# Retention queries of a hybrid decoder layer by seven products that are summed in PSUM

## The chip, the cores and the metric

The kernel runs on one core of one Trainium2 chip. The metric is device time of one execution in microseconds (us), the median of several runs. The core's engines are TensorE (PE in the profile; its weight loads are PEld), VectorE (DVE), ScalarE (ACT), GpSimd (POOL) and SyncE (SP), which here issues DMAs. Each works through its own instructions in order, and semaphores hold an instruction back until what it needs is there.

## The reference

One decoder layer for 512 tokens of width 1024, with 16 learned tokens put in front. Retention, stick-breaking attention and two gates share one input projection; a SwiGLU feed-forward follows. The part that the change touches is the projection of the retention's queries and their rotation:

```python
proj = hn @ w_in                                   # (528, 1024) @ (1024, 11264)
rq, rk, rv, rg, sq, sk, sv, ga, gb = jnp.split(proj, ...)
q_r = rotary(heads(rq, 4), pos) * (256 ** -0.5)    # 4 heads of 256
k_r = rotary(heads(rk, 4), pos)
y_ret = head_groupnorm(retention_chunkwise(q_r, k_r, heads(rv, 4)))
y_ret = (silu(rg) * merge_heads(y_ret)) @ w_ret_out
```

Everything is float32. The queries of a head are a product of 256 x 1024 (weights, transposed) by 1024 x 512 (tokens).

## The kernel before

**Numbers in two parts.** Each operand is held as a high and a low part (`wh`, `wl` for weights, `hT`, `hL` for the normalised tokens), made by `split` (L103): a ScalarE copy into the matmul type and a VectorE subtraction for the rest. A product is then three matmul passes: high by high, high by low, low by high. Weights come from DRAM into `raw` (4 buffers, L120) and are split into `wh`/`wl` (5 pairs, L81); both are reused in turn, so a load waits for a split, and a split waits until TensorE is through with an earlier pair.

**Products of two forms.** `feat_mm` (L142) multiplies weights by tokens with the weights as the stationary operand: for 1024 input rows, 8 row blocks and 3 passes, 24 matmuls into one bank. `seven` (L263) computes a product that is cut in 2 x 2 quarters by seven smaller products in place of eight (Strassen's scheme as Winograd ordered it): it needs sums of weight quarters, s1 to s4, which GpSimd makes (L230 or L258), and sums of token quarters, t1 to t4, which are made once and kept in `th`, `tl`. The retention's values and gate (`tok_seven`, L297) and most of the feed-forward (`feat_seven`, L287) are done so; the partial results are brought together by VectorE in a tile `ub` of SBUF. `feat_quarters` (L221) loads the weights of `feat_seven` in two tiles, makes S1, S2, S3, S4 from them in tiles `x` (S2, S3) and `y` (S1, S4), and splits raw1, x, y and A22, the second half of raw2.

**The retention stage** runs over 4 heads (L1111). `ret_qk` (L990) multiplies the queries: for each half e of the head's 256 columns, `feat_mm` over the 512 tokens into one bank of a pair `pa`. `rotate` (L971) reads the two banks by VectorE and splits the results. Then the keys, over 528 tokens in two pieces of 264 columns, per half e. After that come the scores (`ret_scores`), the gate (`ret_gate`), the weighted values (`ret_pv`), the transposition (`ret_T`), the next head's values (`rv_proj`) and the output projection of this head (`ret_out`, 96 matmuls of 512 columns into banks `pp`). For head 0, `ret_out` copies its banks to `acc` by ScalarE (L1105); for heads 1 and 2 VectorE adds them (L1108).

**What sets the order.** The program is written in the order above, but a scheduler places the instructions on each engine, interleaving what is independent; parts are pinned. So the output projection of head h - 1 stands among the queries and keys of head h, and the gate's first products among the keys. PSUM has pools of two banks `pp`, two `pb`, and two pairs `pa` in this stage.

Of the kernel before, what the change touches and what calls it, by code (L numbers as in the profile page):

```python
# [10 lines left out]
F32 = mybir.dt.float32  # L11
# [23 lines left out]
def hybrid_block(  # L35
# [37 lines left out]
    def bank_a():  # L73
        return ps_a.tile([P, 2, 512], F32, tag="a", name="pa")
# [19 lines left out]
    def mm(*args, **kw):  # L94
        return keep(nc.tensor.matmul(*args, **kw))  # L95
# [43 lines left out]
        cn = src.shape[1]  # L139
        return load_units(src, kn, cn, [(0, kn, c, P) for c in range(0, cn, P)])  # L140

    def feat_mm(dst, unit, xh, xl, kn=KD):  # L142

        wh, wl = unit
        for k in range(kn):
            mm(dst, wh[:, k, :], xh(k), start=(k == 0), stop=False)
            mm(dst, wh[:, k, :], xl(k), start=False, stop=False)
            mm(dst, wl[:, k, :], xh(k), start=False, stop=(k == kn - 1))

    def tok_mm(dst, units, xh, xl, first=True, last=True, k0=0):  # L150

# [63 lines left out]
    def wun_split(v):  # L215
        wh = wun.tile([P, v.shape[1], v.shape[2]], F32R, tag="wh", name="wh")
        wl = wun.tile([P, v.shape[1], v.shape[2]], F32R, tag="wl", name="wl")
        split(wh, wl, v)
        return wh, wl

    def feat_quarters(src, sums, pin=False):  # L221

        raw1, raw2 = raw_of(src[:, 0:P]), raw_of(src[:, P:])
        A11, A12 = raw1[:, 0:KH, :], raw1[:, KH:KD, :]
        A21, A22 = raw2[:, 0:KH, :], raw2[:, KH:KD, :]
        x = sums.tile([P, KD, P], F32, tag="st", name="st")
        y = sums.tile([P, KD, P], F32, tag="st", name="st")
        S1, S2, S3, S4 = y[:, 0:KH, :], x[:, 0:KH, :], x[:, KH:KD, :], y[:, KH:KD, :]
        for d, p, q, op in ((S1, A21, A22, ALU.add), (S2, S1, A11, ALU.subtract), (S3, A11, A21, ALU.subtract), (S4, A12, S2, ALU.subtract)):
            ins = nc.gpsimd.tensor_tensor(d, p, q, op=op)  # L230
            if pin:
                tc.keep_in_program_order(ins)
        f, g = slice(0, KH), slice(KH, KD)
        a, b, c, d = wun_split(raw1), wun_split(x), wun_split(y), wun_split(A22)
        cut = lambda u, k: (u[0][:, k, :], u[1][:, k, :])
        return dict(a11=cut(a, f), a12=cut(a, g), s2=cut(b, f), s3=cut(b, g), s1=cut(c, f), s4=cut(c, g), a22=d)

# [25 lines left out]
    def seven(product, bank1, bank2, ub, after=lambda n: None):  # L263


        n = ub.shape[-1]
        p1 = bank1()
        product(0, p1)
        nc.scalar.activation(ub[:, 1, :], p1, AF.Copy)
        p = bank2()  # L270
        product(1, p[:, 0, :])
        after(1)
        product(2, p[:, 1, :])
        nc.vector.tensor_tensor(ub[:, 0:2, :], p, ub[:, 1:2, :].to_broadcast([P, 2, n]), op=ALU.add)
        p = bank1()
        product(3, p)
        nc.vector.tensor_tensor(ub[:, 2, :], p, ub[:, 1, :], op=ALU.add)
        p = bank1()
        product(4, p)
        nc.vector.tensor_tensor(ub[:, 1:4:2, :], p.rearrange("p (o n) -> p o n", o=1).to_broadcast([P, 2, n]), ub[:, 1:3, :], op=ALU.add)  # L280
        p = bank2()
        product(5, p[:, 0, :])
        product(6, p[:, 1, :])
        after(6)
        nc.vector.tensor_tensor(ub[:, 1:3, :], p, ub[:, 1:3, :], op=ALU.add)
# [11 lines left out]
    def tok_seven(u, tok, ub, **kw):  # L297


        def product(n, dst):  # L300
            a, b = PRODUCTS[n]
            xh, xl = tok.operand(b)
            wh, wl = u[a]
            for s in range(2):
                ts_ = slice(s * P, (s + 1) * P)
                tok_mm(dst[:, s * 256 : (s + 1) * 256], [(wh, wl)], lambda k: xh(k)[:, ts_], lambda k: xl(k)[:, ts_])

        one = iter([bank_p, bank_p, bank_b])
        seven(product, lambda: next(one)(), bank_a, ub, **kw)


    hpool = ctx.enter_context(ExitStack())
# [675 lines left out]
        return s4.tile([P, L], F32R, tag="qk", name="qk", bufs=8)  # L988

    def ret_qk(h):  # L990
        uq = feat_units(w_in[:, O_RQ + DK * h : O_RQ + DK * (h + 1)])
        pq = bank_a()
        for e in range(2):
            feat_mm(pq[:, e, :], uq[e], xtok, ltok)
        q = [(qk_tile(), qk_tile()) for _ in range(2)]
        idf = lambda t: t[:, :T]
        rotate(pq[:, 0, :], pq[:, 1, :], cosT[:, NM:], sinT[:, NM:], idf, [(a[:, :T], b[:, :T]) for a, b in q])
        uk = feat_units(w_in[:, O_RK + DK * h : O_RK + DK * (h + 1)])
        pks = []
        for e in range(2):  # L1000
            pk = bank_a()
            for i in range(2):
                cs = slice(264 * i, 264 * (i + 1))
                feat_mm(pk[:, i, :264], uk[e], lambda k: hT[:, k, cs], lambda k: hL[:, k, cs])
            pks.append(pk[:, :, :264])
        k = [(qk_tile(), qk_tile()) for _ in range(2)]
        two = lambda t: t.rearrange("p (a b) -> p a b", a=2)
        rotate(pks[0], pks[1], two(cosT), two(sinT), two, [(two(a), two(b)) for a, b in k])
        return q, k
# [381 lines left out]
```

## Time and profile before

| | |
|---|---|
| median of 3 runs | 1178.73 us (1178.39 to 1178.78) |
| the profiled execution | 1178.72 us, span 1176.9 us |
| matmuls in the span | 7529 |
| granted TensorE clock, mean | 0.999 |
| retention, query projection of head 0 | from 355.30 us on |
| feed-forward, seven-product part | about 860 to 1040 us |

A row of the page's groups has the line, engine and operation, output <- inputs by the program's names, partitions x elements, the count, then busy time in us, the mean of one in ns, and the idle time of the engine before these instructions with what ended it. A row of the timeline has start and length in us, then the instruction and a count, with idle time and its ender in brackets. A row of windows has, for each engine, busy us and the number of instructions, then the granted clock, the DMA share and GB/s. A row of one line's or tile's instructions has the shortest, the median and the longest duration in ns.

### The profile page before, as it was taken

To read this page: it belongs to the slowest core of one execution; us is meant where nothing else is said; L and a number is where in the kernel's file an instruction comes from. 1 tells how busy PE (TensorE), PEld (TensorE's weight loads), DVE (VectorE), ACT (ScalarE), POOL (GpSimd) and SP (SyncE) were. 2 spreads that over 40 slices of the span, in tenths; PEclk is the share of its full clock that TensorE was granted. 3 is DMA by queue.
4 is the path that set the end of the run, shared out by engine and by line. 5 is a ranking of instruction groups with operands and counts; after the bars stand their busy time and mean duration, and the time that the engine had idled before them with its cause. 6 is when DMAs were issued, how large, how long until landed. Compare 5 with 4: busy or idle time off the path is not lost.

```text
span 1176.9 us, 18856 instructions
## 1 busy us (share of the span) xinstructions
PE 1164.9 (99%) x7529; PEld 1056.3 (90%) x7529; DVE 844.0 (72%) x1120; ACT 532.1 (45%) x899; POOL 333.5 (28%) x358
## 2 busy tenths in 40 slices
PE   9999999999999999999999999999999999999997
PEld 7988999988899998998899898888999999998886
DVE  7488888888577873786586567767799998773333
ACT  6476666666233434434243334335455444442321
POOL 2021112126644403320240200001356676610000
PEclk9999999999999999999999999999999999999999
DMA  7332122222641323115122434344033333353311
GB/s 235 99 99 74 62 72 64 77 77 92 194 148 60 93 90 114 55 53 154 36 82 82 133 90 134 126 160 126 19 108 108 109 108 108 108 162 101 97 36 72
DMA packets 146536, 118.25 MB, mean 100 GB/s; under 512 B 3832, under 2 KB 135168, under 8 KB 146448
## 3 DMA queue, kind: packets, MB, share of 16 engines
q1 hardware_dynamic: 145856, 115.85, 32.5%
q8 instruction: 59, 0.97, 0.4%
q10 hardware_dynamic: 592, 1.20, 0.3%
q14 instruction: 29, 0.24, 0.1%
HBM read 109.96 MB, written 7.08 MB: 99 GB/s over the span
## 4 chain that ended last, share of the span: by engine, by line
PE 92%; DVE 5%; issue 1%; ACT 1%; DMA 0%; POOL 0%; POOLq 0%; DVEq 0%; ACTq 0%
PE pp L95 41%; PE pb L95 20%; PE pa L95 20%; PE pc L95 5%; PE px L95 3%; PE pb L98 3%; DVE wl L101 1%; DVE sm L603 1%; ACT wh L104 1%; DVE sl L101 0%; DMA ysb<-in_x_dram 0%; DVE al L101 0%; DVE kl L101 0%; DVE qb L101 0%; DVE qa L101 0%
## 5 line engine op out<-in xcount | busy, mean ns | idle before, releaser
L101 DVE TENSOR_TENSOR wl<-raw,wh 128x1024 fp32r<-128x1024 f32 x196 | 260.7, 1338 | 60.3 <-ACT wh L104 59.3
L104 ACT ACTIVATE wh<-raw 128x1024 fp32r<-128x1024 f32 x194 | 195.2, 1014 | 203.4 <-PE pa L95 59.5
L95 PE MATMUL pp<-hT,wh 128*128 128x512 f32 (+1 forms) x304 | 112.0, 369 | 0.0
L95 PE MATMUL pp<-hL,wh 128*128 128x512 f32 (+1 forms) x304 | 107.7, 354 | 0.0
L95 PE MATMUL pp<-hT,wl 128*128 128x512 f32 (+1 forms) x304 | 107.6, 354 | 0.0
L258 POOL TENSOR_TENSOR st<-raw 128x512 f32<-128x512 f32 x28 | 44.4, 1608 | 170.3 <-DMA raw<-in_w_in_dram 170.3
L101 DVE TENSOR_TENSOR wl<-st,wh 128x1024 fp32r<-128x1024 f32 x54 | 75.1, 1392 | 13.1 <-ACT wh L104 12.1
L95 PE MATMUL pp<-qk,wh 128*128 128x512 f32 x256 | 80.1, 394 | 0.0
L230 POOL TENSOR_TENSOR st<-raw 128x512 f32<-128x512 f32 x40 | 61.1, 1528 | 50.3 <-DVE wl L101 50.3
L95 PE MATMUL pp<-wh,hT 128*128 128x256 f32 (+1 forms) x240 | 73.9, 309 | 0.1
L95 PE MATMUL pp<-wl,hT 128*128 128x256 f32 (+1 forms) x240 | 73.0, 305 | 0.7 <-DVE wl L101 0.4
L95 PE MATMUL pp<-wh,hL 128*128 128x256 f32 (+1 forms) x240 | 73.0, 305 | 0.2 <-DVE hL L101 0.2
L104 ACT ACTIVATE wh<-st 128x1024 fp32r<-128x1024 f32 x54 | 56.6, 1056 | 35.6 <-PE pp L95 15.6
L95 PE MATMUL pa<-hL,wh 128*128 128x264 f32 (+1 forms) x208 | 66.2, 318 | 0.0
L95 PE MATMUL pa<-hT,wh 128*128 128x264 f32 (+1 forms) x208 | 66.2, 318 | 0.0
L95 PE MATMUL pa<-hT,wl 128*128 128x264 f32 (+1 forms) x208 | 66.1, 318 | 0.0
L603 DVE TENSOR_TENSOR_SCAN sm<-sm,mask 128x528 f32<-128x528 f32 (+1 forms) x64 | 54.8, 857 | 14.3 <-ACT sm L600 13.5
L95 PEld LDWEIGHTS pp<-hT,wl 128*128 128x128 f32 x304 | 57.2, 188 | 8.4
L613 POOL CAST mg<-sp 128x32 fp32r<-128x32 f32 x32 | 7.5, 233 | 197.6 <-DVE sp L604 153.7
L95 PEld LDWEIGHTS pp<-hT,wh 128*128 128x128 f32 x304 | 57.3, 188 | 5.8
L95 PEld LDWEIGHTS pp<-hL,wh 128*128 128x128 f32 x304 | 57.4, 189 | 5.3
L95 PEld LDWEIGHTS pp<-qk,wh 128*128 128x128 f32 x256 | 47.7, 188 | 10.7
(346 smaller groups left out, 3680.3 us busy)
## 6 DMA issues: line engine op xcount, KB each, us to landing
raw<-in_w_in_dram SPq DMA_DIRECT2D x88, 512.0 KB, 4.2
raw<-in_w_ffn_in_dram SPq DMA_DIRECT2D x44, 512.0 KB, 3.8
raw<-in_w_ffn_out_dram SPq DMA_DIRECT2D x22, 512.0 KB, 3.6
raw<-in_w_ret_out_dram SPq DMA_DIRECT2D x16, 512.0 KB, 3.4
raw<-in_w_sb_out_dram SPq DMA_DIRECT2D x8, 512.0 KB, 3.9
raw<-in_w_out_dram SPq DMA_DIRECT2D x8, 512.0 KB, 4.0
ysb<-in_x_dram SPq DMA_DIRECT2D x4, 512.0 KB, 7.1
gb_d<-go SPq DMA_DIRECT2D x8, 256.0 KB, 2.0
```

What stands on the lines that cost most here:

```text
L95: return keep(nc.tensor.matmul(*args, **kw))
L98: return keep(nc.tensor.transpose(dst, src, idn))
L101: return nc.vector.tensor_tensor(lo, src, hi.bitcast(F32), op=ALU.subtract)
L104: ins = nc.scalar.activation(hi, src, AF.Copy)
L230: ins = nc.gpsimd.tensor_tensor(d, p, q, op=op)
L258: nc.gpsimd.tensor_tensor(d[:, k : k + 2], p[:, k : k + 2], q[:, k : k + 2], op=op)
L603: nc.vector.tensor_tensor_scan(rev, rev, mask[:, r0:][:, ::-1], 0.0, op0=ALU.mult, op1=ALU.max)
L613: nc.gpsimd.tensor_copy(g[:, two, 0:NM], m)
```

## The change

The queries alone go over to seven products; the keys stay as they were. `ret_qk` loads the query weights by `feat_quarters`, with the sums y (S1, S4) split ahead of x (S2, S3), and calls a new function, `feat_chain`. This does not bring the partial results together in SBUF with an add for each, as `seven` does. It lets TensorE go on adding into the same PSUM bank ("a" or "b") and copies the bank out by ScalarE at each point at which the running sum is one of the quarters or a part of one: bank "a" holds a11 b11, then with s2 t2, then with s3 t3, then with a22 t4. Bank "b" holds s1 t1, then with s4 b22. The product a12 b21 has a bank of its own. The results are four quarters of a SBUF tile `ub` (the one buffer that `seven` also uses), from which `rotate` now reads. The first half of the keys, `keys(0)`, is written between the products, the second after the queries' rotation.

```diff
-    def feat_mm(dst, unit, xh, xl, kn=KD):
+    def feat_mm(dst, unit, xh, xl, kn=KD, first=True, **kw):
 
         wh, wl = unit
         for k in range(kn):
-            mm(dst, wh[:, k, :], xh(k), start=(k == 0), stop=False)
-            mm(dst, wh[:, k, :], xl(k), start=False, stop=False)
-            mm(dst, wl[:, k, :], xh(k), start=False, stop=(k == kn - 1))
+            mm(dst, wh[:, k, :], xh(k), start=(first and k == 0), stop=False, **kw)
+            mm(dst, wh[:, k, :], xl(k), start=False, stop=False, **kw)
+            mm(dst, wl[:, k, :], xh(k), start=False, stop=(k == kn - 1), **kw)
...
-        a, b, c, d = wun_split(raw1), wun_split(x), wun_split(y), wun_split(A22)
+        a = wun_split(raw1)
+        if s1_first:
+            c, b = wun_split(y), wun_split(x)
+        else:
+            b, c = wun_split(x), wun_split(y)
+        d = wun_split(A22)
...
+    def feat_chain(u, tok, q, u22, beside=None):
+        banks = {}
+
+        def product(name, bank, more=False):
+            a, b = name
+            feat_mm(banks[bank], u[a], *tok.operand(b), KH, first=not more, skip_group_check=True)
+
+        def add(d, p):
+            nc.vector.tensor_tensor(d, p, d, op=ALU.add)
+
+        (q11, q12), (q21, q22) = [[q[:, e, H * t : H * (t + 1)] for t in range(2)] for e in range(2)]
+
+        def rest():
+            banks["c"] = bank_p()[:, :H]
+            product(("a12", "b21"), "c")
+            add(q11, banks["c"])
+
+        banks["a"] = bank_a()[:, 0, :H]
+        product(("a11", "b11"), "a")
+        nc.scalar.activation(q11, banks["a"], AF.Copy)
+        if beside:
+            rest()
+        banks["b"] = bank_p()[:, :H]
+        product(("s1", "t1"), "b")
+        nc.scalar.activation(q22, banks["b"], AF.Copy)
+        product(("s2", "t2"), "a", True)
+        nc.scalar.activation(q12, banks["a"], AF.Copy)
+        product(("s4", "b22"), "b", True)
+        add(q12, banks["b"])
+        product(("s3", "t3"), "a", True)
+        nc.scalar.activation(u22, banks["a"], AF.Copy)
+        add(q22, u22)
+        (beside or rest)()
+        product(("a22", "t4"), "a", True)
+        nc.scalar.activation(q21, banks["a"], AF.Copy)
...
     def ret_qk(h):
-        uq = feat_units(w_in[:, O_RQ + DK * h : O_RQ + DK * (h + 1)])
-        pq = bank_a()
-        for e in range(2):
-            feat_mm(pq[:, e, :], uq[e], xtok, ltok)
+        uq = feat_quarters(w_in[:, O_RQ + DK * h : O_RQ + DK * (h + 1)], s4, s1_first=True)
+        uk = feat_units(w_in[:, O_RK + DK * h : O_RK + DK * (h + 1)])
+        pks = []
+
+        def keys(e):
+            pk = bank_a()
+            pks.append(pk[:, :, :264])
+            for i in range(2):
+                cs = slice(264 * i, 264 * (i + 1))
+                feat_mm(pk[:, i, :264], uk[e], lambda k: hT[:, k, cs], lambda k: hL[:, k, cs])
+
+        pq = s4.tile([P, 4, 512], F32, tag="ub", name="ub", bufs=1)
+        feat_chain(uq, tokens, pq, pq[:, 2, :H], lambda: keys(0))
...
-        uk = feat_units(w_in[:, O_RK + DK * h : O_RK + DK * (h + 1)])
-        pks = []
-        for e in range(2):
-            pk = bank_a()
-            for i in range(2):
-                cs = slice(264 * i, 264 * (i + 1))
-                feat_mm(pk[:, i, :264], uk[e], lambda k: hT[:, k, cs], lambda k: hL[:, k, cs])
-            pks.append(pk[:, :, :264])
+        keys(1)
```

How the change moves instructions, at three places. First TensorE in head 0, right behind the values of that head; before, the first matmul of each block (`wh_4186` and `wh_4190` are the two halves of the query weights, `wh_4265` and `wh_4269` those of the keys, `pp_4501` is the gate):

```order
L95 MATMUL pa_4194<-hT_83,wh_4186 128x512
L95 MATMUL pa_4194<-hT_83,wh_4190 128x512
L95 MATMUL pa_4273<-hT_83,wh_4265 128x264
L95 MATMUL pp_4501<-wh_4397,hT_83 128x256
L95 MATMUL pa_4322<-hT_83,wh_4269 128x264
```

and after, again the first matmul of each block (`pa_4221` is bank "a", `pp_4249` bank "b", `pp_4235` bank "c"; `wh_4192` holds a11 and a12, `wh_4196` y, `wh_4200` x, `wh_4204` a22; `pa_4303` and `wh_4212` are the first half of the keys, `pa_4383` the second):

```order
L95 MATMUL pa_4221<-hT_83,wh_4192 128x256
L95 MATMUL pp_4235<-hT_83,wh_4192 128x256
L95 MATMUL pp_4249<-th_94,wh_4196 128x256
L95 MATMUL pa_4303<-hT_83,wh_4212 128x264
L95 MATMUL pa_4221<-th_94,wh_4200 128x256
L95 MATMUL pp_4249<-hT_83,wh_4196 128x256
L95 MATMUL pa_4221<-th_94,wh_4204 128x256
L95 MATMUL pp_4562<-wh_4458,hT_83 128x256
L95 MATMUL pa_4383<-hT_83,wh_4216 128x264
```

Two blocks of 24 matmuls of 512 columns became seven of 12 of 256. The 48 of the first key half are spread among them: 2 stand ahead of s2 (`wh_4200`), 10 behind it, 2 ahead of s3, 34 ahead of a22.

Second, ScalarE in head 0, after, from the first key split to the last copy out of bank "a" (L337, L342, L344, L348 and L352 are the five copies of `feat_chain`; `rvm` and `vs` belong to the learned tokens' values; `wh_4458` to `wh_4480` are the gate's weights):

```order
L104 ACTIVATE wh_4212<-raw_4208 128x1024
L1000 ACTIVATE vs_3952<-pb_4149 16x256
L337 ACTIVATE ub_4220<-pa_4221 128x256
L104 ACTIVATE wh_4216<-raw_4210 128x1024
L104 ACTIVATE rvm_3886<-vs_3952 16x512
L342 ACTIVATE ub_4220<-pp_4249 128x256
L1011 ACTIVATE rvm_3886<-rvm_3886 16x512
L344 ACTIVATE ub_4220<-pa_4221 128x256
L348 ACTIVATE ub_4220<-pa_4221 128x256
L104 ACTIVATE wh_4476<-st_4466 128x1024
L104 ACTIVATE wh_4480<-st_4467 128x1024
L352 ACTIVATE ub_4220<-pa_4221 128x256
```

Before, no copy of the queries stood in this queue. Now each stands behind a split or a copy of something else, the first behind the key split and two value copies, the last behind two splits of the gate's sums (`st`).

Third, VectorE in head 2, where the output projection of head 1 (`acc`) stands among the queries' weights; before (`raw_6240` and `raw_6242` are the two query tiles):

```order
L1108 TENSOR_TENSOR acc_3901<-pp_6130,acc_3901 128x512
L101 TENSOR_TENSOR wl_6181<-raw_6174,wh_6180 128x1024
L101 TENSOR_TENSOR wl_6245<-raw_6240,wh_6244 128x1024
L101 TENSOR_TENSOR vl_6092<-ub_5873,vh_6091 128x2x256 x2
L101 TENSOR_TENSOR wl_6249<-raw_6242,wh_6248 128x1024
L958 TENSOR_TENSOR vs_5874<-pb_6071,vs_5874 16x256
L1108 TENSOR_TENSOR acc_3901<-pp_6144,acc_3901 128x512
L1108 TENSOR_TENSOR acc_3901<-pp_6158,acc_3901 128x512
L101 TENSOR_TENSOR rvm_3886<-vs_5874,rvm_3886 16x512
```

and after (`wl_6377` is y's low half, `wl_6381` x's; L1153 is the add that was L1108):

```order
L1153 TENSOR_TENSOR acc_3901<-pp_6252,acc_3901 128x512
L101 TENSOR_TENSOR wl_6303<-raw_6296,wh_6302 128x1024
L101 TENSOR_TENSOR wl_6373<-raw_6362,wh_6372 128x1024
L101 TENSOR_TENSOR vl_6214<-ub_5995,vh_6213 128x2x256 x2
L1001 TENSOR_TENSOR vs_5996<-pb_6193,vs_5996 16x256
L1153 TENSOR_TENSOR acc_3901<-pp_6266,acc_3901 128x512
L101 TENSOR_TENSOR wl_6377<-st_6367,wh_6376 128x1024
L101 TENSOR_TENSOR rvm_3886<-vs_5996,rvm_3886 16x512
L1153 TENSOR_TENSOR acc_3901<-pp_6280,acc_3901 128x512
L101 TENSOR_TENSOR wl_6381<-st_6366,wh_6380 128x1024
L1153 TENSOR_TENSOR acc_3901<-pp_6306,acc_3901 128x512
```

The fourth add (`pp_6158`, now `pp_6280`) followed the third directly; now the low half of y, which waits for GpSimd's sums by way of ScalarE, and the learned tokens' values stand ahead of it.

2 lines of the change are left out of this document (1 added, 1 removed).

## The prediction, made before the changed kernel had run

> **What bounds the kernel now.** I read the page first, then the windows of the retention stage, then single rows where the change acts.
>
> ```profile
> span 1176.9 us, 18856 instructions
> PE 1164.9 (99%) x7529; PEld 1056.3 (90%) x7529; DVE 844.0 (72%) x1120; ACT 532.1 (45%) x899; POOL 333.5 (28%) x358
> PE 92%; DVE 5%; issue 1%; ACT 1%; DMA 0%; POOL 0%; POOLq 0%; DVEq 0%; ACTq 0%
> core 0: us, PE busy (x) PEld busy (x) DVE busy (x) ACT busy (x) POOL busy (x), PEclk, DMA share, GB/s
> 355.00:640.00 285.00, 284.79 (x1924) 262.00 (x1923) 204.70 (x260) 111.18 (x151) 81.52 (x60) 1.00 0.27 83
> ```
>
> TensorE (PE) is busy 99% of the span, and carries 92% of the chain that ended last. The last row is a stretch of some three retention heads: TensorE stands still for 0.2 of 285 us, at full granted clock. So matmul time taken out shortens the run one for one, and any new wait of TensorE lengthens it one for one. Each other engine has room there on average (VectorE 80 us, ScalarE 174, GpSimd 203); only the moment at which something is ready can cost.
>
> **The matmuls.** Their durations mislead, so I count from start to start.
>
> ```profile
> L95 PE MATMUL pa<-hT,wh 128*128 128x512 f32 x64 | 25.2, 393 | 0.0
> 355.30 0.39 PE L95 MATMUL pa<-hT,wh 128*128 128x512 f32 x1
> 366.41 0.28 PE L95 MATMUL pa<-hT,wh 128*128 128x264 f32 x1
> L95 PE MATMUL pb<-nT,wh 128*128 128x256 f32 x144 | 40.6, 282 | 0.0
> 860.00:1040.00 180.00, 180.00 (x1511) 180.00 (x1510) 162.77 (x159) 83.87 (x103) 116.49 (x72) 1.00 0.36 106
> ```
>
> The query projection of head 0 begins at 355.30 and the keys at 366.41: 48 matmuls of 512 columns in 11.11 us, 231 ns each. The window in the feed-forward stage holds only matmuls of 256 columns, in the same seven-product form: 1511 in 180.00 us, 119.1 ns each. The new projection has 7 products x 4 row blocks x 3 passes = 84 of these: 10.0 us. **Saved: 11.11 - 10.0 = 1.1 us a head, 4.4 us in four heads.** The keys keep their 96 matmuls a head; they are only cut into pieces around the products.
>
> The Trainium skill (TensorE: Matmul & The Clock Gate, Back-to-back issue gap and LDWEIGHTS) speaks against this: in a stream of weight loads and matmuls the spacing is set by both, and a load costs its columns over 1.2, 107 ns for 128. Were that load added to each matmul, 36 more loads a head would eat the saving, an estimate of 3.9 us by that page against 1.1. The trace differs: 1510 loads stand beside the 1511 matmuls at 119 ns, so the load is in that figure already.
>
> **The other work.** Per head the change adds four GpSimd operations of 512 elements, 3.5 splits of 1024 in place of 2, five ScalarE copies of 256 out of PSUM and three VectorE adds of 256.
>
> ```profile
> L230 POOL TENSOR_TENSOR st<-raw x40: 1285/1674/1759, 828.2 to 1030.4; 128x512 f32<-128x512 f32 x40
> L230 POOL TENSOR_TENSOR st<-st,raw x20: 1282/1296/1622, 829.5 to 1029.2; 128x512 f32<-128x512 f32 x20
> L230 POOL TENSOR_TENSOR st<-raw,st x20: 1739/2278/2299, 832.8 to 1032.1; 128x512 f32<-128x512 f32 x20
> L101 DVE TENSOR_TENSOR wl<-st,wh 128x1024 fp32r<-128x1024 f32 x54 | 75.1, 1392 | 13.1 <-ACT wh L104 12.1
> L104 ACT ACTIVATE wh<-st 128x1024 fp32r<-128x1024 f32 x54 | 56.6, 1056 | 35.6 <-PE pp L95 15.6
> L269 ACT ACTIVATE ub<-pp 128x512 f32<-128x512 f32 x6 | 3.6, 597 | 0.1
> L957 ACT ACTIVATE vs<-pb 16x256 f32<-16x256 f32 x5 | 1.8, 370 | 0.1
> L277 DVE TENSOR_TENSOR ub<-pp,ub 128x512 f32<-128x512 f32 x6 | 4.1, 686 | 0.1
> ```
>
> GpSimd's sums, the same four operations as in the feed-forward stage: 2 x 1.67 + 1.30 + 2.28 = 6.9 us (minima 5.6, maxima 7.4). ScalarE: 1.5 x 1.06 for splits and five copies. A copy of 256 columns is not in the trace; it lies between 0.37 (256 on 16 partitions) and 0.60 (512), and I take 0.60, since that row too reads 128 partitions of PSUM. Together 4.6 us. VectorE: 1.5 x 1.39 + 3 x at most 0.69 = 4.2. All of this lies beside TensorE on average; the question is the places where TensorE waits for it.
>
> **Head 0** has no output projection of an earlier head to fill in. Here I replay the chain.
>
> ```profile
> 339.86 0.40 SPq L121 DMA_DIRECT2D raw<-in_w_in_dram  x1
> DMA to landing us min/median/max: 4.9/5.1/5.4
> 351.84 0.69 DVE L101 TENSOR_TENSOR vl<-ub,vh 128x512 fp32r<-128x512 f32 x1 [0.70 <-ACT vh L104]
> 353.94 1.22 DVE L285 TENSOR_TENSOR ub<-pa,ub 128x1024 f32<-128x1024 f32 x1
> 355.41 1.14 ACT L104 ACTIVATE vh<-ub 128x512 fp32r<-128x512 f32 x2
> ```
>
> The second weight tile is issued at 339.86 and lands by 345.3 (the landings of that stretch); 6.9 of sums give 352.2. ScalarE splits y (S1 and S4) by 353.2, a value copy and x (S2 and S3) follow by 354.9. VectorE's low halves of y, of a value quarter and of x, then the last sum of the values (1.22) end at 357.9. Behind it ScalarE has two value copies (1.14), the key split (1.06), a meta copy (0.37) and then q11's copy out of bank "a", which is done at about 361.1. TensorE, from 355.30, has a11, a12 and s1, 36 matmuls, and two of the keys: ready for s2 on bank "a" at 359.8. **It waits 1.2 us** (nothing if the sums take their minima; up to 3 if VectorE is held up too). The other hand-overs have a product or a piece of keys (1.4 us or more) to cover a copy of 0.6.
>
> **Heads 1 to 3** have the output projection of the head before among the chain. Its sums are taken out of two banks by ScalarE (head 1) or by VectorE's adds (heads 2, 3), and the new splits stand ahead of these in both queues.
>
> ```profile
> 541.08 0.37 SPq L121 DMA_DIRECT2D raw<-in_w_in_dram  x1
> raw<-in_w_in_dram SPq DMA_DIRECT2D x88, 512.0 KB, 4.2
> 544.42 1.21 DVE L285 TENSOR_TENSOR ub<-pa,ub 128x1024 f32<-128x1024 f32 x1
> 546.15 0.68 DVE L1108 TENSOR_TENSOR acc<-pp,acc 128x512 f32<-128x512 f32 x1
> 549.88 0.63 PE L95 MATMUL pp<-qk,wh 128*128 128x512 f32 x2
> ```
>
> Head 2: issue 541.08, landing 545.3, sums 552.2, y split 553.3, its low half 554.6, the meta values' low half 555.3, the fourth add 556.0. TensorE began that fourth product (12 matmuls) at 549.88. Now, from 549.7: 12 of these, 10 of a11, 12 of the fifth, 2 of s2, and at 556.6 the sixth product wants that bank: 0.6 spare. The third add comes, by the same queue (1.21, 0.69, 0.68, two splits, two value halves, 0.41, 0.68), at 552.3 and is wanted at 553.6. So I take no wait, with 0 to 1.8 as bounds (next part).
>
> **Sum**, against the profiled execution's own 1178.72 (span 1176.9 and 1.8 around it; the median of the runs shown is 1178.73): -4.4 + 1.2 = -3.2, **1175.5 us**.
>
> **Rivals.**
>
> *VectorE loses time to GpSimd's new sums.*
>
> ```profile
> 352.79 1.23 DVE L101 TENSOR_TENSOR wl<-raw,wh 128x1024 fp32r<-128x1024 f32 x1 [0.26 <-ACT wh L104]
> 354.59 3.53 POOL L258 TENSOR_TENSOR st<-raw 128x512 f32<-128x512 f32 x2 [16.98 <-DMA raw<-in_w_in_dram]
> 356.89 3.47 DVE L101 TENSOR_TENSOR vl<-ub,vh 128x512 fp32r<-128x512 f32 x2
> 358.08 3.44 POOL L258 TENSOR_TENSOR raw<-raw 128x512 f32<-128x512 f32 x2
> 360.29 2.31 DVE L101 TENSOR_TENSOR wl<-raw,wh 128x1024 fp32r<-128x1024 f32 x1
> ```
>
> With GpSimd idle a value half takes 0.69 and a weight half 1.23; beside GpSimd's rows two of the first take 3.47 and one of the second 2.31: 3.2 us lost in 5.7. The skill (SBUF — State Buffer, Who interferes with whom) gives the reason: a VectorE instruction with two SBUF inputs contends with a GpSimd instruction that reads SBUF, one with at most one does not. The trace agrees. In head 2 just such halves fill VectorE's queue from 545.3 on. A loss of 3.1 puts the third add at 555.4, 1.8 late. With this in heads 2 and 3 and head 0's 1.2: 1178.7 - 4.4 + 4.8 = **1179.1**. Against it: in the window of the feed-forward stage the same sums run every 10 us beside a VectorE at 90%, the weight halves average 1.39, and TensorE never stops.
>
> *A bank copy behind a split that waits for GpSimd (slower).* In head 0 the last copy, q21's, stands in ScalarE's queue behind two splits of the gate's weights, the first of which needs six of GpSimd's pieces.
>
> ```profile
> L258 POOL TENSOR_TENSOR st<-raw x28: 1283/1302/2332, 354.6 to 666.9; 128x512 f32<-128x512 f32 x28
> ```
>
> The gate's second tile takes the slot of the second query tile, free at about 358.6; it lands at 362.8. Six pieces at 1.30 end at 370.6, two splits and the copy at 373.3. TensorE wants that bank, for the second half of the keys, at 355.3 + 10.0 + 5.9 (keys) + 1.2 + 2.9 (24 of the gate) = 375.3. At the maximum, 2.33, the pieces end at 376.8 and the copy at 379.5: 4.2 late. It decides from 1.64 a piece on. Heads 1 to 3 lie between 0 and 4.2 each; I take 0.8, near the low end, since there 96 matmuls of the output projection (22 us at 231 ns) run among the chain and give GpSimd that much more time: 1178.7 - 4.4 + 1.2 + 4.2 + 2.4 = **1182.1**.
>
> *The durations are the cost.* 84 x 0.282 against 48 x 0.393 would be 4.8 us more a head, **1198**. The starts quoted above exclude it nearly.
>
> **How the numbers follow.** Forecast 1175.5: 0.55. VectorE's loss, 1179.1: 0.33. Copy behind the split, 1182.1: 0.11. Durations: 0.01. Faster by over 0.2% (2.4 us, about what a measurement of this kernel can tell from no change) is the first, 0.55; within it the second, 0.33; slower the last two, 0.12. The range runs from no wait at all (1174.3, and 0.4 for the spacing's own uncertainty) to the first rival: 1173.9 to 1179.2. Within the forecast alone it is 1173.9 to 1176.4.
>
> **What would show it.** The query chain's matmuls at 119 ns from start to start; TensorE idle before s2 in head 0, ended by ScalarE's copy into ub, about 1 us; none before the output projection's products in heads 2 and 3. There, a wait ended by the add into acc, with weight halves of 2 us ahead of it, is the first rival; a wait before the second half of the keys, ended by the last copy into ub, the second. A spacing well over 119 ns in the chain would make the saving itself wrong.

## The result, and the profile after

The changed kernel takes **1185.18 us** (median of 4 runs, 1184.73 to 1185.55), beside 1178.76 (1178.39 to 1178.86) for the kernel before on the same chip: a ratio of 1.0055, 95% interval 1.0037 to 1.0072. The forecast was 1175.5. The profiled execution took 1185.55 us.

The page of the changed kernel, its span, its engines and the shares of the chain that ended last:

```profile
span 1183.8 us, 19227 instructions
PE 1163.2 (98%) x7673; PEld 1060.5 (90%) x7673; DVE 884.6 (75%) x1140; ACT 545.7 (46%) x927; POOL 365.9 (31%) x374
PE 78%; DVE 12%; issue 4%; ACT 2%; DMA 2%; POOL 2%; POOLq 0%; DVEq 0%; ACTq 0%
```

TensorE's busy time fell by 1.7 us, and yet the span grew by 6.9. VectorE (DVE) has 40.6 us more, and its share of the chain went from 5% to 12%. What TensorE waited for between 350 and 740 us, the retention heads (engine, tile and line <- who ended the wait: us in total, number, the longest). Before, this view is empty for the same stretch. After:

```profile
PE pp L95 <- DVE acc L1153: 2.5, 2, 1.3
PE pb L95 <- DVE qk L101: 1.7, 1, 1.7
PE pa L95 <- DVE wl L101: 1.1, 1, 1.1
PE pa L95 <- DVE rt L1025: 1.0, 2, 0.9
PE pp L95 <- ACT wh L104: 0.5, 1, 0.5
PE pb L95 <- ACT qk L104: 0.2, 1, 0.2
PE pa L95 <- ACT ub L337: 0.2, 1, 0.2
```

Of 7.2 us of waits VectorE ended 6.3, at four kinds of place: the add of the output projection into `acc` (heads 2 and 3), the low half of a rotated key ahead of the scores (head 1), a low half of query weights (head 1), and the rotation, which holds a bank pair. The last row is the wait that was forecast for head 0, at a sixth of its size.

The list shows too little of each wait. The record of a matmul of 256 columns lasts 0.28 us and the next one starts 0.12 us after it, so the first 0.16 us of a stop count as busy, and a short stop does not show at all. Counted from start to start (all that is over 0.1 us above the usual spacing), TensorE loses 11.5 us between 350 and 740 us, and lost 1.0 before.

Two whole heads (1 and 2) from the first matmul of head 1 that reads `xm` to the first of head 3, as a row of windows, before and then after:

```profile
433.67:641.54 207.87, 207.79 (x1378) 189.85 (x1377) 142.20 (x182) 79.79 (x108) 52.74 (x40) 1.00 0.28 84
```

```profile
435.53:647.43 211.90, 207.07 (x1449) 192.07 (x1448) 165.04 (x192) 86.99 (x122) 68.51 (x48) 1.00 0.27 83
```

VectorE has ten instructions more here, which at its mean of before (142.20 / 182 = 0.78) would be 7.8 us; it has 22.8 us more. What grew is seen in the timeline of head 2, before and then after: the head's first `xm` matmul, as a marker, and VectorE's rows some ten us behind it.

```profile
537.71 0.28 PE L95 MATMUL pb<-wh,xm 128*48 128x256 f32 x1
...
545.55 0.68 DVE L101 TENSOR_TENSOR vl<-ub,vh 128x512 fp32r<-128x512 f32 x1
546.75 2.35 DVE L101 TENSOR_TENSOR wl<-raw,wh 128x1024 fp32r<-128x1024 f32 x2
549.01 1.28 DVE L101 TENSOR_TENSOR vl<-ub,vh 128x512 fp32r<-128x512 f32 x2
551.35 0.41 DVE L958 TENSOR_TENSOR vs<-pb,vs 16x256 f32<-16x256 f32 x1
551.69 0.67 DVE L1108 TENSOR_TENSOR acc<-pp,acc 128x512 f32<-128x512 f32 x1
```

```profile
541.97 0.28 PE L95 MATMUL pb<-wh,xm 128*48 128x256 f32 x1
...
549.80 1.76 DVE L101 TENSOR_TENSOR vl<-ub,vh 128x512 fp32r<-128x512 f32 x1
551.49 0.68 DVE L1153 TENSOR_TENSOR acc<-pp,acc 128x512 f32<-128x512 f32 x1
552.09 3.95 DVE L101 TENSOR_TENSOR wl<-raw,wh 128x1024 fp32r<-128x1024 f32 x2
555.96 2.39 DVE L101 TENSOR_TENSOR vl<-ub,vh 128x512 fp32r<-128x512 f32 x2
558.27 0.41 DVE L1001 TENSOR_TENSOR vs<-pb,vs 16x256 f32<-16x256 f32 x1
558.61 0.67 DVE L1153 TENSOR_TENSOR acc<-pp,acc 128x512 f32<-128x512 f32 x1
```

Beside these stand GpSimd's new sums (L230), and behind the last add TensorE:

```profile
549.72 3.00 POOL L230 TENSOR_TENSOR st<-raw 128x512 f32<-128x512 f32 x2 [21.39 <-DMA raw<-in_w_in_dram]
552.68 2.28 POOL L230 TENSOR_TENSOR st<-st,raw 128x512 f32<-128x512 f32 x1
555.04 2.16 POOL L230 TENSOR_TENSOR st<-raw,st 128x512 f32<-128x512 f32 x1
559.33 0.74 PE L95 MATMUL pp<-qk,wh 128*128 128x512 f32 x2 [1.31 <-DVE acc L1153]
```

From 549.72 to 557.20 both engines read SBUF. Two weight halves take 3.95 us where they took 2.35, value halves 1.76 and 2.39 (for two) where one took 0.68 and two 1.28. Only the add at 551.49, which reads a bank of PSUM, kept its 0.68. The next add is late by these, and TensorE with it.

I counted this over the trace. An instruction of VectorE is called **lengthened** if it took over 0.3 us longer than the shortest with the same line, tiles and shapes in the stretch. From 355 to 740 us there are 21 before (16.4 us in all) and 45 after (42.6 us), and each one of these, in both kernels, ran beside an instruction of GpSimd. All read two operands in SBUF; of those with an operand in PSUM (the adds into `acc`, into `ub`, the rotation out of `pa`) none was lengthened.

### The profile page after: what moved, and what is told of

It is laid out like the page before. It is cut to its first block, busy times and chain, and to the rows that moved or that the text cites. A ratio compares the mean times of both kernels' runs of the same rounds, so it can differ in the third digit from the quotient of the medians.

```text
span 1183.8 us, 19227 instructions
## 1 busy us (share of the span) xinstructions
PE 1163.2 (98%) x7673; PEld 1060.5 (90%) x7673; DVE 884.6 (75%) x1140; ACT 545.7 (46%) x927; POOL 365.9 (31%) x374
## 4 chain that ended last, share of the span: by engine, by line
PE 78%; DVE 12%; issue 4%; ACT 2%; DMA 2%; POOL 2%; POOLq 0%; DVEq 0%; ACTq 0%
PE pp L95 37%; PE pb L95 19%; PE pa L95 12%; DVE wl L101 5%; PE pc L95 5%; PE px L95 3%; PE pb L98 3%; DMA raw<-in_w_in_dram 1%; ACT wh L104 1%; DVE sm L646 1%; DVE vl L101 1%; DVE qk L101 1%; POOL st L230 1%; POOL ts L196 1%; DVE rt L1021 1%
## 5 line engine op out<-in xcount | busy, mean ns | idle before, releaser
L101 DVE TENSOR_TENSOR wl<-raw,wh 128x1024 fp32r<-128x1024 f32 x196 | 272.8, 1398 | 50.7 <-ACT wh L104 48.9
L95 PE MATMUL pp<-hT,wh 128*128 128x512 f32 (+2 forms) x336 | 120.8, 360 | 0.0
L95 PE MATMUL pp<-hT,wl 128*128 128x512 f32 (+2 forms) x336 | 116.6, 347 | 0.0
L95 PE MATMUL pp<-hL,wh 128*128 128x512 f32 (+2 forms) x336 | 116.5, 347 | 0.0
L230 POOL TENSOR_TENSOR st<-raw 128x512 f32<-128x512 f32 x48 | 74.5, 1555 | 122.3 <-DMA raw<-in_w_in_dram 71.7
L101 DVE TENSOR_TENSOR wl<-st,wh 128x1024 fp32r<-128x1024 f32 x62 | 91.2, 1475 | 17.6 <-ACT wh L104 17.3
L104 ACT ACTIVATE wh<-st 128x1024 fp32r<-128x1024 f32 x62 | 64.9, 1055 | 45.4 <-POOL st L230 18.6
L263 POOL TENSOR_TENSOR st<-raw 128x512 f32<-128x512 f32 x28 | 45.1, 1633 | 74.0 <-DMA raw<-in_w_in_dram 66.1
L646 DVE TENSOR_TENSOR_SCAN sm<-sm,mask 128x528 f32<-128x528 f32 (+1 forms) x64 | 54.9, 857 | 14.3 <-ACT sm L643 13.5
L101 DVE TENSOR_TENSOR gl<-gt,gh 128x512 fp32r<-128x512 f32 x22 | 15.9, 732 | 51.3 <-ACT gh L104 51.2
L230 POOL TENSOR_TENSOR st<-raw,st 128x512 f32<-128x512 f32 x24 | 51.7, 2155 | 0.3
L95 PE MATMUL pp<-qk,wl 128*128 128x512 f32 x128 | 49.9, 394 | 0.0
```

The source lines that it names most:

```text
L101: return nc.vector.tensor_tensor(lo, src, hi.bitcast(F32), op=ALU.subtract)
L104: ins = nc.scalar.activation(hi, src, AF.Copy)
L263: nc.gpsimd.tensor_tensor(d[:, k : k + 2], p[:, k : k + 2], q[:, k : k + 2], op=op)
L646: nc.vector.tensor_tensor_scan(rev, rev, mask[:, r0:][:, ::-1], 0.0, op0=ALU.mult, op1=ALU.max)
```

## The experiments

Four theories, named in the expectations, some by their first letter. **Lock**: VectorE is held up while GpSimd reads SBUF, and TensorE waits for it. **Work**: VectorE's added low halves and adds are too much by themselves. **Delay**: ScalarE's splits wait for GpSimd's sums, and bank copies stand behind them. **Hand-over**: the two banks that are summed up and copied in turn are the trouble. All kernels start from the changed one, except where said.

### 1. No sums of query weights

```diff
-        for d, p, q, op in ((S1, A21, A22, ALU.add), ...):
+        for d, p, q, op in () if s1_first else ((S1, A21, A22, ALU.add), ...):
...
-            c, b = wun_split(y), wun_split(x)
+            c, b = wun_split(raw2), wun_split(raw1)
```

> The four GpSimd sums of each head's query weights are left out: the splits read the two weight tiles themselves in place of y and x, so the queries are not the reference's, while every matmul, split, copy and VectorE add of the changed kernel is still there. Theories for the 6.4 us that the change cost (TensorE's waits grew by 10.8 us against 4.4 us of matmul time saved). L, the lock: VectorE is slowed while GpSimd reads SBUF. W, the work: VectorE has more to do, by 1.5 weight halves and three adds a head, and that alone makes it late. D, the delay: the splits wait for the sums, and what stands behind them in ScalarE's and VectorE's queues waits too. L: 1175 to 1178. D: 1175 to 1178 as well. W: 1183 to 1186.

Measured: 1179.90 us, ratio to before 1.0008 (0.9998 to 1.0017), over the range of lock and delay and under that of work. The waits for `acc` and for `wl` are gone; of the larger ones are left

```profile
PE pb L95 <- DVE qk L101: 1.7, 1, 1.7
PE pa L95 <- DVE rt L1025: 1.3, 4, 0.7
```

So the query sums cost 5.3 us (1185.2 - 1179.9), and 5.5 more are lost without them against the 1174.4 that the matmul saving alone would give. Neither lock nor delay as put explains that rest.

### 2. Sums made, but not read

The sums stay on GpSimd; the splits read the unsummed weights (the second half of the edit above alone).

> As the run without sums, in the same order on every engine, but GpSimd makes the sums as in the changed kernel and nothing reads them: their occupation of SBUF stays, the wait for them is gone. The splits read the two weight tiles, so the queries are not the reference's. L: 1182 to 1186, like the changed kernel. D: 1175 to 1178, like the run without sums. W: 1183 to 1186. The difference from the run without sums is the price of the lock by itself.

Measured: 1188.46 us, ratio 1.0081 (1.0063 to 1.0099), 8.6 us over the kernel without sums and over the lock's range. No split waits for a sum here, and the order of the instructions is that of the kernel without sums, so the delay theory falls as the cause of these 8.6. In TensorE's waits the `acc` row is larger than in the changed kernel (2.5):

```profile
PE pp L95 <- DVE acc L1153: 4.3, 2, 2.2
```

That it is slower than the changed kernel by 3.3 us was not expected. Its trace shows two reasons. In heads 2 and 3 a low half of query weights, which need not wait for the sums here, stands ahead of the add that TensorE waits for; in the changed kernel it stands behind it. Head 2:

```profile
558.29 1.21 DVE L101 TENSOR_TENSOR wl<-raw,wh 128x1024 fp32r<-128x1024 f32 x1
559.76 1.27 DVE L1153 TENSOR_TENSOR acc<-pp,acc 128x512 f32<-128x512 f32 x2
```

With this the `acc` row grew by 1.8 us. The other reason is the granted clock, which in the profiled execution was halved for a while, as a row of windows shows (the third figure from the end is the clock):

```profile
561.40:564.80 3.40, 3.40 (x10) 2.62 (x9) 1.44 (x2) 0.16 (x1) 0.00 (x0) 0.50 0.39 116
```

Of the four runs two had a mean granted clock of 0.999 and took 1187.4 and 1187.5 us; the others, with 0.998 (the profiled one) and 0.995, took 1189.4. At the higher clock the sums that nobody reads cost 7.6 us.

### 3. The query sums on VectorE

```diff
-            ins = nc.gpsimd.tensor_tensor(d, p, q, op=op)
+            ins = (nc.vector if s1_first else nc.gpsimd).tensor_tensor(d, p, q, op=op)
```

> The same sums, correct, made by VectorE in place of GpSimd: four operations of 512 elements at about 0.69 us, 2.8 us more of VectorE a head, no reads of GpSimd for them. L: 1178 to 1182, since VectorE's own 2.8 us replace a loss of about 3 and the sums are done sooner. D: 1177 to 1181, since the sums take 2.8 us rather than 6.9. W: 1187 to 1192.

Measured: 1182.51 us, ratio 1.0032 (1.0020 to 1.0043), 0.5 us over the lock's range. VectorE has four instructions more a head and the kernel is 2.7 us faster than the changed one; by the work theory as first put it should have been slower. Still 2.6 us are lost against the kernel without query sums.

### 4. Seven products without the chain in the banks

```diff
-        feat_chain(uq, tokens, pq, pq[:, 2, :H], lambda: keys(0))
+        feat_seven(uq, tokens, pq.rearrange("p a n -> p (a n)")[:, 0:1024].rearrange("p (a n) -> p a n", a=4))
+        keys(0)
```

The first half of the keys is no longer spread among the products either.

> The seven products of the queries put together as in the feed-forward, by VectorE's adds into SBUF over banks of their own, with one ScalarE copy; no running sums in PSUM. Correct. It adds VectorE work of about 2 us a head and takes four ScalarE copies away. W: 1188 to 1194. L and D: 1184 to 1188. If instead the hand-over of the banks to ScalarE were the cost (a fourth theory, H): 1176 to 1180.

Measured: 1191.11 us, ratio 1.0104 (1.0088 to 1.0120): within the work theory's range, over that of lock and delay. The hand-over theory falls. But part of this is the granted clock. In the profiled execution (1191.62 us) it was halved in three stretches of 3.4 us, from 384.1, 599.1 and 708.4 us on; the first:

```profile
384.10:387.50 3.40, 3.33 (x14) 3.00 (x15) 3.40 (x5) 2.08 (x3) 0.00 (x0) 0.50 0.12 22
```

Counted from start to start, TensorE loses 4.6 us in these stretches, and 12.8 by stops in the rest of the heads, where the changed kernel loses 11.5. The mean clock of the four runs was 0.994 to 0.997, that of the changed kernel's runs 0.998 and 0.999. So only some 1.2 us of the 5.9 by which this form is slower are shown to be stops; whether it also brought the clock down is not shown.

### 5. No sums at all in the heads

The first edit, and also no sums of the gate and value weights of heads 1 to 3:

```diff
-        for d, p, q, op in ((y, A11, A21, ALU.subtract), ...):
+        for d, p, q, op in () and ((y, A11, A21, ALU.subtract), ...):
...
-        u["s2"], u["s3"], u["s1"] = wun_split(x), wun_split(y), wun_split(A21)
+        u["s2"], u["s3"], u["s1"] = wun_split(A11), wun_split(A21), wun_split(A21)
```

> The sums of the query weights and of the gate and value weights (heads 1 to 3) are all left out; the splits read the unsummed quarters in their place, so neither the queries nor gates nor values are the reference's. GpSimd is then nearly idle in the heads. Lock theory: between 355 and 740 us the changed kernel has 45 VectorE instructions that took over 0.3 us longer than the shortest of their form (42.6 us in all), each of them beside a GpSimd instruction; without the query sums 33 (31.5 us) are left, and their waits are what keeps that kernel 5 us above the 1174.4 us that the matmul saving alone would give. Here under 3 are left, and the time is 1174 to 1176 us. Work theory (VectorE's added low halves and the rotation out of SBUF are too much by themselves): 1179 to 1180.5 us, as without the query sums.

Measured: **1173.56 us**, ratio 0.9954 (0.9936 to 0.9971), 0.4 us under the lock's range. TensorE waits for nothing between 350 and 740 us, counted from start to start too, and no instruction of VectorE is lengthened. The same two heads:

```profile
432.23:637.23 205.00, 205.00 (x1450) 191.70 (x1449) 141.11 (x192) 87.47 (x122) 4.61 (x8) 1.00 0.28 86
```

VectorE does the same 192 instructions as in the changed kernel in 141.1 us in place of 165.0. Its added low halves and adds are all here, and cost nothing: the added work by itself falls as the cause. What was left after the first experiment, 6.3 us, came from the sums of the gate and the values, which the change did not touch. No run makes these and leaves them unread, so no edit tells lock and delay apart for them; but in experiment 1 none of TensorE's listed waits is ended by a split of weights.

### 6. All sums on VectorE

The third edit, and `nc.vector` for the gate and value sums as well.

> The sums of the query weights and of the gate and value weights (heads 1 to 3) are made by VectorE in place of GpSimd. Per head VectorE gets 16 more instructions of 0.68 us than with the query sums alone, 11 us, and loses the 8 us by which GpSimd still lengthens its instructions there. Lock theory: VectorE's busy time between 355 and 740 us goes from 324.6 to about 336 us of 385, with under 3 lengthened instructions; a wait is then set by work alone, 1177 to 1182 us. Work theory: 12 us more of VectorE's work costs 1184 to 1188 us.

Measured: 1187.25 us, ratio 1.0066 (1.0050 to 1.0082): within the work theory's range, over the lock theory's.

```profile
437.53:650.10 212.57, 207.83 (x1450) 191.66 (x1449) 164.69 (x233) 87.66 (x122) 6.09 (x8) 1.00 0.27 82
```

No instruction is lengthened, but VectorE does the sums itself, and its busy time is that of the changed kernel (164.7 and 165.0 us). With the same time taken, by waiting for GpSimd or by adding, TensorE loses about as much. VectorE's time counts, whichever way it is filled; the lock is one way to fill it. The profiled execution also had the clock at 0.50 for 3.4 us, from 425.2 us on, ahead of these two heads; the one run of four with a mean clock of 0.999 took 1185.15 us, the changed kernel's time.

### 7. The kernel before, without gate and value sums

The second part of edit 5, applied to the kernel before.

> The kernel before, queries by whole products, with the sums of the gate and value weights (heads 1 to 3) left out, so that gates and values are not the reference's. Both theories: no change, 1178.2 to 1179.2 us, since TensorE has 0.2 us of gaps in the heads of the kernel before, though VectorE's 21 lengthened instructions (16.4 us) go. Anything under 1177.5 us would say that the lock costs the kernel before as well.

Measured: 1177.57 us, ratio 0.9988 (0.9978 to 0.9998), 0.6 us under the forecast: the old sums cost the kernel before something as well, in stops too short for the list of waits (1.0 us from start to start before, none here).

```profile
433.58:640.83 207.25, 207.25 (x1377) 189.64 (x1376) 134.95 (x182) 80.07 (x108) 4.38 (x8) 1.00 0.28 85
```

The same gate and value sums that cost 6.3 us with the change cost 1.2 without it. This pair also gives the saving with nothing else in it: 1177.57 - 1173.56 = 4.0 us, and 207.25 - 205.00 = 2.25 for two heads.

### 8. Fills in place of the query sums

The splits read the unsummed weights, as in experiment 2.

```diff
-            ins = nc.gpsimd.tensor_tensor(d, p, q, op=op)
+            ins = nc.gpsimd.memset(d, 0.0) if s1_first else nc.gpsimd.tensor_tensor(d, p, q, op=op)
```

> In place of the four sums of the query weights GpSimd fills the same tiles with zeros, which nobody reads; the splits read the unsummed weights, so the queries are not the reference's. Against the kernel whose sums were made and not read (1188.5 us) and the one without sums (1179.9 us). If what holds VectorE up is GpSimd reading two operands in SBUF: 1179 to 1181 us, and no VectorE instruction beside a fill is lengthened. If any GpSimd access to SBUF does it: in proportion to the fills' duration, up to 1185 to 1189 us if they last as long as the sums.

Measured: 1180.05 us, ratio 1.0012 (1.0003 to 1.0022), as without query sums. Rows of the timeline in head 0, GpSimd's fills and what VectorE did beside them:

```profile
401.25 2.04 POOL L230 MEMSET st<- 128x512 f32 x4 [1.21 <-DVE wl L101]
401.04 0.68 DVE L101 TENSOR_TENSOR sl<-tm,sh 128x512 fp32r<-128x512 f32 x1
402.78 0.89 DVE L101 TENSOR_TENSOR sl<-tm,sh 128x384 fp32r<-128x384 f32 x2 [0.26 <-ACT sh L104]
```

The halves `sl`, with two operands in SBUF, keep their 0.68 and 0.89 beside the fills (the kernel without sums has the same durations). Nine such halves ran beside fills between 355 and 740 us, and none was lengthened: GpSimd's fills, which only write SBUF, did not hold VectorE up. The fills are shorter than the sums (0.53 us each, against 1.3 to 2.3) and come at another time, so this says what a write does, not what a fill in the sums' place would cost.

### 9. Sums in halves

```diff
-            for k in range(0, KH, 2):
-                nc.gpsimd.tensor_tensor(d[:, k : k + 2], p[:, k : k + 2], q[:, k : k + 2], op=op)
+            for k in range(KH):
+                nc.gpsimd.tensor_tensor(d[:, k], p[:, k], q[:, k], op=op)
```

The query sums are cut in two in the same way.

> All sums as in the changed kernel and on GpSimd, but in instructions of half the size (256 elements a partition in place of 512), for the query weights and for the gate and value weights of heads 1 to 3. In the changed kernel a VectorE instruction beside a sum is longer by about 1.1 us, which is nearly one whole sum of 1.27 us. Lock theory, in the form that VectorE waits until the GpSimd instruction that runs is through: the mean lengthening falls to 0.4 to 0.6 us; if the number of lengthened instructions between 355 and 740 us stays near 45, VectorE loses about 20 us of the 42.6, and the time is 1177 to 1181 us. If the two engines just share bandwidth for as long as both work: no change in the 42.6 us, 1184 to 1187 us.

Measured: 1187.87 us, ratio 1.0076 (1.0061 to 1.0091), over both ranges. The mechanism came out as forecast, and the time did not: 38 lengthened instructions with 20.0 us in all, 0.53 each. But the waits have changed hands. TensorE's two largest rows, and in head 2 ScalarE and GpSimd:

```profile
PE pa L95 <- ACT ub L339: 3.3, 3, 1.6
PE pa L95 <- DVE rt L1027: 3.0, 4, 1.0
```

```profile
550.40 5.29 POOL L232 TENSOR_TENSOR st<-raw 128x256 f32<-128x256 f32 x4 [21.26 <-DMA raw<-in_w_in_dram]
555.66 2.33 POOL L232 TENSOR_TENSOR st<-st,raw 128x256 f32<-128x256 f32 x2
557.95 1.43 POOL L232 TENSOR_TENSOR st<-raw,st 128x256 f32<-128x256 f32 x2
559.41 1.06 ACT L104 ACTIVATE wh<-st 128x1024 fp32r<-128x1024 f32 x1 [6.19 <-POOL st L232]
562.76 0.38 ACT L339 ACTIVATE ub<-pa 128x256 f32<-128x256 f32 x1
```

The set of sums takes 9.0 us (550.40 to 559.38) where it took 7.5. ScalarE stands still 6.2 us before the split of these sums, and the bank copy into `ub` that TensorE needs is queued behind it. GpSimd loses much of what VectorE no longer does, as if the two took turns: in the two heads of the table below the lengthening of VectorE is 13.7 us less than in the changed kernel, and GpSimd is busy 18.7 us longer. Some 7 of these 18.7 are the halves' own cost (an estimate from 40 sums, 0.73 us for a half and 1.28 for a whole where VectorE stands still). The delay theory, fallen as the main cause for whole sums, holds here.

### 10. The normalised rows on ScalarE

```diff
-            nc.vector.tensor_scalar(yn, y, mv[:, 0:1], rs, op0=ALU.subtract, op1=ALU.mult)
+            nb = s4.tile([P, 1], F32, tag="nb", name="nb")
+            nc.vector.tensor_scalar(nb, mv[:, 0:1], rs, -1.0, op0=ALU.mult, op1=ALU.mult)
+            nc.scalar.activation(yn, y, AF.Identity, bias=nb, scale=rs)
```

> The changed kernel, but the normalised attention rows (yn, four in a head, read from the banks) are made by ScalarE out of VectorE's mean and deviation, with one small VectorE instruction for the offset; the sums stay on GpSimd as they are. VectorE loses four instructions of about 0.67 us a head and gets four of about 0.1: some 2.2 us a head less, 9 of 322.6 us between 355 and 740 us. If what counts is VectorE's time in the head, whatever fills it (lengthened or not): TensorE's gaps fall by a quarter to a half, 1181 to 1184 us. If only the lengthened instructions themselves count: 1184 to 1186 us.

Measured: 1186.06 us, ratio 1.0061 (1.0045 to 1.0078), at the upper end of the second range: no gain over the changed kernel, though VectorE's sum of durations from 355 to 740 us fell from 322.6 to 314.5. None of the waits listed for the changed kernel is ended by those rows. This fits that VectorE's time ahead of the waits counts, not its time in the head as a whole, and limits what experiment 6 says.

### 11. Both edits, 9 and 10

> Both of the two edits: the sums in instructions of half the size and the normalised rows on ScalarE. Lock theory: the two add up, VectorE has about 30 us less to do between 355 and 740 us than in the changed kernel, near the 290 us of the kernel before, and the time is 1174 to 1178 us, under that of the kernel before. Otherwise 1181 to 1185 us.

Measured: 1189.59 us, ratio 1.0090 (1.0075 to 1.0105), over both ranges. VectorE is down to 294.9 us, near the kernel before, and the kernel is slower still: of TensorE's 11.4 us of listed waits ScalarE ends 7.8, and VectorE's rotation the other 3.6.

### 12. Query sums on VectorE, the other sums in halves

Edit 3 and the part of edit 9 that is shown.

> The query sums on VectorE, as in the kernel at 1182.5 us, and the gate and value sums of heads 1 to 3 left on GpSimd in instructions of half the size. From the two runs by themselves: with the query sums on VectorE 34 instructions are lengthened (31.7 us between 355 and 740 us), and no split of query weights waits for GpSimd; halves brought the mean lengthening from 0.95 to 0.53 us, but made GpSimd's sums longer, so that ScalarE's splits waited for them. Lock theory, if the halves' delay falls on the query splits alone: 31.7 goes to 15 to 18 us, the waits at the scores and the accumulator shrink, 1177 to 1181 us, at or under the kernel before. If the gate splits are delayed in the same way: no gain or a loss, 1182 to 1186 us.

Measured: 1182.85 us, ratio 1.0034 (1.0022 to 1.0046), the same as with edit 3 alone and in the second range. The lengthening fell to 12.7 us, and ScalarE's splits of the gate's sums came late in return (0.9 us in head 0), with the bank pair held by the rotation longer (3.0 in place of 1.8 us in all):

```profile
PE pa L95 <- DVE rt L1025: 3.0, 4, 1.0
PE pp L95 <- ACT wh L104: 0.9, 1, 0.9
```

No version tried that computes the queries by seven products, sums and all, beats the kernel before.

### Heads 1 and 2 side by side

From marker to marker as above; VectorE's busy time by the row of windows, lengthened instructions counted as said.

| kernel | time, us | two heads, us | VectorE busy, us | lengthened | by, us |
|---|---|---|---|---|---|
| 7, whole queries, no sums | 1177.6 | 207.3 | 135.0 | 0 | 0 |
| before | 1178.8 | 207.9 | 142.2 | 6 | 3.4 |
| 5, no sums at all | 1173.6 | 205.0 | 141.1 | 0 | 0 |
| 1, no query sums | 1179.9 | 208.9 | 158.1 | 15 | 14.7 |
| 8, fills | 1180.1 | 209.1 | 157.3 | 14 | 13.7 |
| 3, query sums on VectorE | 1182.5 | 209.7 | 161.9 | 14 | 13.5 |
| changed | 1185.2 | 211.9 | 165.0 | 24 | 24.3 |
| 6, all sums on VectorE | 1187.3 | 212.6 | 164.7 | 0 | 0 |
| 9, sums in halves | 1187.9 | 211.8 | 153.3 | 20 | 10.6 |

From 5 to the changed kernel TensorE's products are the same, and the two heads and VectorE's time grow together. In 6 VectorE's time is its own work, and in 9 most of the loss is at ScalarE.

## Why the prediction was wrong

**The saving was right.** 119 ns a matmul with its weight load, 1.1 us a head: the pair of experiments 5 and 7, without waits in either, gives 4.0 us in four heads against the 4.4 forecast. That weight loads would eat it did not come true: kernel 5 makes 1449 loads in its two heads, 73 more than kernel 7, and is the faster one.

**Head 0: right in place, wrong in size.** The wait before s2 was forecast at 1.2 us and is 0.2: the copy out of bank "a" ended at 360.1 us, not 361.1, mainly since the low halves ahead of it took 1.22 us each where 1.39 was reckoned, and the copy itself 0.38 where 0.60 was. Two others came that the replay did not follow: 0.5 for a split of ScalarE and 0.9 for the rotation.

**The step that failed is "Heads 1 to 3 ... I take no wait, with 0 to 1.8 as bounds".** In head 2 the replay was right in all but VectorE's durations. It had the third add done at 552.3, 14.6 us after the marker (537.71), and wanted by TensorE at 553.6, 15.9 after it. In the trace the add ends at 559.28 (558.61 + 0.67), 17.3 after its marker (541.97), and TensorE goes on at 17.4. The queue ahead of it was the one forecast; its weight and value halves were longer. From start to start TensorE loses 8.4 us in heads 1 to 3 (3.8, 2.9 and 1.7), where the sum had 0, and 3.1 in head 0, where it had 1.2. With 4.0 us saved, and the 1.0 that the kernel before lost itself, 11.5 us make 1185.3; measured are 1185.2.

**The first rival had the mechanism and gave it too few places.** It priced one late add in each of heads 2 and 3 (1.8 us; measured 1.3 at most) and came to 1179.1. It left out, first, that the loss also meets `wl` of head 1's queries and the scores' `qk`; and second, the old sums. In the kernel before these lengthen 6 instructions of VectorE in two heads; with the change and no new sums, 15. The rotation shows why. Before, it read the queries from PSUM, and the keys' part of it had time to spare; after, it ends later and reads `ub` in SBUF. Rows of before, then of the kernel without query sums, both in head 1:

```profile
483.62 0.71 DVE L978 TENSOR_TENSOR rt<-pa,sinT 128x528 f32<-128x528 f32 x1 [4.28 <-PE pa L95]
490.39 0.71 DVE L101 TENSOR_TENSOR qk<-rt,qk 128x528 fp32r<-128x528 f32 x1 [0.71 <-ACT qk L104]
```

```profile
478.67 1.78 DVE L1021 TENSOR_TENSOR rt<-ub,sinT 128x512 f32<-128x512 f32 x1
480.38 0.68 DVE L1025 TENSOR_TENSOR rt<-ub,sinT 128x512 f32<-128x512 f32 x1
492.86 1.79 DVE L1027 TENSOR_TENSOR rt<-rt 128x528 f32<-128x528 f32 x1
496.80 1.77 DVE L101 TENSOR_TENSOR qk<-rt,qk 128x528 fp32r<-128x528 f32 x1
498.62 0.63 PE L95 MATMUL pb<-qk 128*16 128x512 f32 x2 [1.66 <-DVE qk L101]
```

Before, VectorE itself waited 4.3 us for TensorE in the keys' rotation, and began the last low half of the keys at 490.39, just ahead of GpSimd's next sums (from 490.56 on). With the change it begins that half at 496.80, amid these sums (from 488.02 on), and takes 1.77 us for it; TensorE waits for it. That slack covered the old sums, and the prediction did not name it. Of the 11.6 us between the changed kernel and the one without sums, 5.3 go with the new sums, taken out first, and 6.3 with the old ones.

**The argument against that rival misled.** In the feed-forward stage the same sums run beside a busy VectorE and TensorE never stops. That is so, but the retention heads have short hand-overs from VectorE to TensorE, and it was these that had to be looked at. The averages ("80 us of room") said nothing about them either, as the text itself had warned.

**The second rival** did not happen in the changed kernel: no row of its waits is ended by the last copy. Its mechanism, a bank copy behind a split that waits for GpSimd, makes the largest wait of experiment 9, at the first copy of the chain in place of the last.

**What stays open:** whether the old sums act by the lock alone, what starts the stretches of half clock, and how 5's time could be had with sums. Loads that bring the query weights earlier, or sums made ahead of the head, were not tried.

## What to carry to other kernels

Before giving GpSimd elementwise work, list what VectorE does in the same microseconds: every VectorE instruction with two SBUF operands there may grow by most of a GpSimd instruction, and a result that moves from PSUM to SBUF joins that list. Price the slack that old work already leans on, not only the new work: here half of the loss came from sums that had cost next to nothing. Halving GpSimd's instructions moved the loss here, and did not remove it. And before two forms of a kernel are compared to a few microseconds, look at the granted clock of each run: it made most of the difference between experiment 4 and the changed kernel.

## What the runs showed of the hardware

A VectorE instruction with two SBUF operands beside a GpSimd sum of 512 elements can be longer by up to about 1.1 us, whatever its own length: 0.68 becomes 1.78, 1.21 becomes 2.31. In the changed kernel 27 of the 45 lengthened ones grew by that much, the others by 0.4 to 1.0. With GpSimd instructions of 256 elements it is 0.53 on average. GpSimd's sum grows in turn, from 1.3 to 2.3 us. The Trainium skill (SBUF — State Buffer, SBUF: two separate sides) calls the shared port pair an exclusive lock that one side holds for a whole instruction; the halving in experiment 9 agrees, and so do the fills of experiment 8, which read nothing and held nothing up. The granted clock was 0.50 in single stretches of 3.4 us in the profiled executions of experiments 2, 4 and 6, and TensorE lost about 1.5 us in each. All five came within 1.5 us of the end of a stop of TensorE of 0.9 to 2.6 us; but the changed kernel has stops of 1.2 to 1.8 us without one, so a stop alone does not bring it about.
